# A hybrid retention / gated DeltaNet layer: the conditioning stage without GpSimd, with a matmul plan in slots, and the first value product in one pass

## The chip, the cores and the metric

The kernel runs on one core of a Trainium2 chip. The metric is the time of one execution on the device in microseconds, the median of several runs. The engines are TensorE (PE; its weight loads are listed as PEld), VectorE (DVE), ScalarE (ACT), GpSimd (POOL) and SyncE (SP), whose queue issues most of the transfers.

## The reference

One decoder layer on x of 1024 tokens by 2048 features, all in f32. Cut to what matters here:

```python
mod = silu(c) @ w_ada + b_ada                 # w_ada 2048 x 6144
shift, scale, gate = split(mod, 3)
hin = x * (1 + scale) + shift
proj = hin @ w_in                             # w_in 2048 x 7184
r_q, r_k, r_v, r_g, g_qkv, g_g, g_a, g_b = split(proj)
ret_out = groupnorm(retention(rot(r_q), rot(r_k), r_v)) * silu(r_g)         # 4 heads
gdn_out = rmsnorm(gated_delta(conv_silu(g_qkv), g_a, g_b)) * silu(g_g)      # 8 heads
y = concat(ret_out, gdn_out) @ w_out
out = layernorm(2 ** 0.25 * x + gate * y)
```

## The kernel before

Every large product keeps f32 precision with three matmuls in a faster format: an operand is split into a rounded part (`hi`, a cast on ACT) and its rest (`lo`, a subtraction), and hi x hi, hi x lo and lo x hi are summed in PSUM.

**The conditioning stage** (L139 to L356) makes the modulated input, transposed, in 16 blocks `kt` of 128 features, and does a part of `proj` beside it. The order is written out by hand for every engine (`manual_schedule`), in a loop of steps `s_`. In step `s_`:

- `load_w` brings the shift and scale columns of `w_ada` for block `s_`: four tiles `wa` of four rows `r` each, 256 KB per transfer, seven buffers. `load_x` brings the block of `x` for the next step (two buffers). All are issued by SP.
- `accumulate` (L196) forms silu(c)-weighted sums on DVE: 16 products of 128x256 (`NV = 16`), each added to one of two accumulators, and one closing sum of both (L205). Four products (`NS`) come first, the others are spread over six slots of the step.
- `reduce` (L207) sums the accumulator over its 128 partitions on PE, by a matmul with a column of ones for shift and one for scale. `modulate` (L214) adds the bias on DVE (L217, it waits for the reduction), scales `x` on ACT (L221), casts `h_hi` on ACT (L222) and subtracts to `h_lo` on POOL (L223). It works on block `s_ - 1`: in steps 1 and 2 ahead of the products, later after the first slot.
- `transpose_x` (L227) turns the block of `x` by eight PE transposes, in slots 1 and 3.
- `first_mms` (L267) does items of `proj`. An item is one block `kt` of one of two groups of columns: group 0 is `RG` (second half), `GK` and 272 columns of `RV` with the two DeltaNet gates, the latter for two of eight token tiles; group 1 is `RQ`, `RK` and `RG` (first half). An item has three tiles `t`, 18 matmuls. `TURNS` says in which order the groups use the three PSUM tiles; at the end of a turn `evict` copies the sums out (ACT) or adds them to those of an earlier turn (DVE, L298). Items are taken at `RATE = 2.0` a step, at the earliest two steps behind their block. `load_item` and `split_item` bring and split an item's weights ahead of it: the cast on ACT, the rest `w_lo` on POOL (`split` with `G`, L95), three weight buffers.

Step 16 holds two items and a last step four, all behind the last block's sum.

**After the stage**, `gemm_v(0, ...)` (L440) finishes the 272 value and gate columns for the token tiles 2 to 7. It does so in two passes of three tiles, each over all 16 blocks; each pass loads and splits the same weights in eight units (`w_unit`, L98, the rest on DVE), and uses two PSUM tiles of two banks. The evicted parts of the stage go through gates, convolution and rotary embedding on DVE, ACT and POOL meanwhile. Then follow the eight DeltaNet heads and three more retention heads: `gemm_cm` (L435) and `gemm_v` for the products, with the heads' small work spread between the matmuls, and the output product (L1065).

## Time and profile before

| | us |
|---|---|
| median of 3 runs | 1992.31 (1990.45 to 1999.22) |
| the profiled execution | 1987.55 |
| its span | 1985.7 |
| PE busy | 1879.0 (95%) |
| DVE busy | 1186.3 (60%) |
| ACT busy | 559.7 (28%) |
| POOL busy | 260.2 (13%) |

The span is the time from the first to the last instruction. A transfer counts as issued by a queue and landed later; the DMA share is the mean busy share of the 16 DMA engines, and a share above 1 occurs because packets overlap. A wait for several things is put down to the one that came last. PEclk is the granted TensorE clock: 1.00 is 2.4 GHz and 0.50 is 1.2 GHz. Successive matmuls overlap, so the price of one in a row is read from the start of one to the start of the next.

### The profile page before, as it was taken

Reading aid. Unit: us, or ns where it says so; the run is one execution under the profiler, and the core shown is the slowest. Engines: PE = TensorE matmul, PEld = TensorE weight load, DVE = VectorE, ACT = ScalarE, POOL = GpSimd, SP = SyncE. Lnnn points to the kernel's source line nnn. Section 1 sums busy time; section 2 is a strip of 40 time slices with the busy share of each in tenths; the row PEclk is TensorE's granted clock in tenths of the full one; section 3 lists DMA queues with packets and bytes.
Section 4 is the critical chain, followed back from the end, with each engine's and each line's share of the span. In section 5 each row is a group of like instructions: output and inputs, shape, how many; then the busy total and the mean of one; then the engine's idle time right before and its main releaser. Section 6 shows DMA issues by size and latency. Waiting matters only on the chain.

```text
span 1985.7 us, 28065 instructions
## 1 busy us (share of the span) xinstructions
PE 1879.0 (95%) x10272; PEld 1579.6 (80%) x10272; DVE 1186.3 (60%) x2950; ACT 559.7 (28%) x1251; POOL 260.2 (13%) x214
## 2 busy tenths in 40 slices
PE   4888899999999999999999999999999999998996
PEld 3766777787888878787878898898898878886885
DVE  7997646666575757475575752544542534458557
ACT  2433223332323232322323231211211232224221
POOL 2445202000000010000000010010010100005102
PEclk9899999999999999999999999999999999999998
DMA  9997322222221213222221241144141167345532
GB/s 272 265 262 202 114 71 72 59 67 59 59 60 51 72 49 77 49 68 58 70 58 47 72 135 52 42 146 131 43 133 49 46 206 234 118 139 176 189 111 91
DMA packets 296811, 212.29 MB, mean 107 GB/s; under 512 B 46985, under 2 KB 256474, under 8 KB 295906
## 3 DMA queue, kind: packets, MB, share of 16 engines
q1 hardware_dynamic: 294050, 202.12, 36.0%
q0 software_dynamic: 2624, 8.39, 1.2%
q8 instruction: 80, 1.31, 0.3%
q14 instruction: 57, 0.47, 0.1%
HBM read 191.54 MB, written 18.92 MB: 106 GB/s over the span
## 4 chain that ended last, share of the span: by engine, by line
PE 74%; DMA 6%; DVE 4%; issue 2%; POOL 1%; ACT 1%; SPq 0%; ACTq 0%; DVEq 0%; POOLq 0%
PE pg L435 44%; PE po L1065 14%; PE pg L468 7%; DMA gb<-gc_d 4%; DMA graw<-in_w_ada_dram 1%; DMA mixed<-mxr 1%; PE ps L753 1%; PE ps L896 1%; PE ps L563 1%; PE ps L890 1%; POOL z L1121 1%; POOL yc L877 1%; PE ps L562 1%; PE ps L912 1%; PE ps L911 1%
## 5 line engine op out<-in xcount | busy, mean ns | idle before, releaser
L435 PE MATMUL pg<-h_hi,w_hi 128*128 128x512 f32 x1376 | 451.9, 400 | 0.2 <-DVE gab L480 0.2
L435 PE MATMUL pg<-h_hi,w_lo 128*128 128x512 f32 x1376 | 449.3, 400 | 0.1
L435 PE MATMUL pg<-h_lo,w_hi 128*128 128x512 f32 x1376 | 448.3, 400 | 0.0
L94 ACT CAST w_hi<-w_raw 128x512 fp32r<-128x512 f32 (+3 forms) x244 | 150.2, 616 | 646.9 <-PE pg L435 451.2
L1065 PE MATMUL po<-wr,ms 128*128 128x512 f32 x1380 | 319.2, 393 | 8.2 <-DVE wr L1012 5.7
L1065 PEld LDWEIGHTS po<-wr,ms 128*128 128x128 f32 x1380 | 260.7, 189 | 64.8 <-DVE wr L1012 7.5
L435 PEld LDWEIGHTS pg<-h_hi,w_hi 128*128 128x128 f32 x1376 | 256.5, 189 | 49.3 <-ACT w_hi L94 1.7
L435 PEld LDWEIGHTS pg<-h_hi,w_lo 128*128 128x128 f32 x1376 | 256.9, 189 | 48.6 <-DVE w_lo L95 1.1
L435 PEld LDWEIGHTS pg<-h_lo,w_hi 128*128 128x128 f32 x1376 | 257.6, 189 | 47.6
L95 DVE TENSOR_TENSOR w_lo<-w_raw,w_hi 128x512 fp32r<-128x512 f32 (+1 forms) x211 | 150.3, 713 | 218.0 <-ACT w_hi L94 213.2
L1012 DVE TENSOR_TENSOR wr<-raw,wr 128x512 fp32r<-128x512 f32 x116 | 88.2, 763 | 111.8 <-ACT wr L1010 106.7
L468 PE MATMUL pg<-w_lo,h_hi 128*128 128x256 f32 (+1 forms) x480 | 138.1, 288 | 6.2 <-DVE w_lo L95 6.2
L468 PE MATMUL pg<-w_hi,h_hi 128*128 128x256 f32 (+1 forms) x480 | 138.7, 289 | 3.1 <-ACT w_hi L94 2.5
L468 PE MATMUL pg<-w_hi,h_lo 128*128 128x256 f32 (+1 forms) x480 | 137.9, 287 | 0.0
L201 DVE SCALAR_TENSOR_TENSOR acc<-wa,cs,acc 128x256 f32<-128x256 f32 x224 | 125.8, 623 | 4.2 <-DMA wa<-in_w_ada_dram 3.7
L1010 ACT CAST wr<-raw 128x512 fp32r<-128x512 f32 x116 | 71.8, 621 | 160.0 <-PE po L1065 148.8
L468 PEld LDWEIGHTS pg<-w_lo,h_hi 128*128 128x128 f32 x480 | 92.2, 192 | 7.6 <-DVE w_lo L95 7.5
L468 PEld LDWEIGHTS pg<-w_hi,h_hi 128*128 128x128 f32 x480 | 92.2, 192 | 6.1 <-ACT w_hi L94 4.9
L468 PEld LDWEIGHTS pg<-w_hi,h_lo 128*128 128x128 f32 x480 | 92.2, 192 | 0.0
L626 DVE SCALAR_TENSOR_TENSOR yc<-pg,cw,yc 128x1023 f32<-128x1023 f32 (+2 forms) x69 | 88.3, 1279 | 2.9 <-ACT yc L623 1.9
L415 DVE SCALAR_TENSOR_TENSOR gacc<-graw,cs,gacc 128x512 f32<-128x512 f32 x60 | 47.4, 790 | 49.4 <-DMA graw<-in_w_ada_dram 48.5
L223 POOL TENSOR_TENSOR h_lo<-xT,h_hi 128x1024 fp32r<-128x1024 f32 x16 | 48.9, 3057 | 91.4 <-ACT h_hi L222 79.0
(242 smaller groups left out, 2356.3 us busy)
## 6 DMA issues: line engine op xcount, KB each, us to landing
w_raw<-in_w_in_dram SPq DMA_DIRECT2D x212, 256.0 KB
wa<-in_w_ada_dram SPq DMA_DIRECT2D x128, 256.0 KB
raw<-in_w_out_dram SPq DMA_DIRECT2D x128, 256.0 KB
graw<-in_w_ada_dram SPq DMA_DIRECT2D x64, 256.0 KB
xs<-in_x_dram SPq DMA_DIRECT2D x16, 512.0 KB
gb<-gc_d SPq DMA_DIRECT2D x32, 256.0 KB
raw<-mixed SPq DMA_DIRECT2D x32, 256.0 KB
z<-in_x_dram SPq DMA_DIRECT2D x32, 256.0 KB
```

The costliest lines, as they stand in the source:

```text
L94: S.copy(hi[:, :n], raw[:, :n])
L95: (eng_l or V).tensor_tensor(out=lo[:, :n], in0=raw[:, :n], in1=hi[:, :n].bitcast(F32), op=ALU.subtract)
L201: V.scalar_tensor_tensor(out=a, in0=wr, scalar=cs[:, r:r + 1], in1=zero.broadcast_to([P, 2 * P]) if r < 2 else a, op0=ALU.mult, op1=ALU.add)
L223: G.tensor_tensor(out=h_lo, in0=xT, in1=h_hi.bitcast(F32), op=ALU.subtract)
L415: V.scalar_tensor_tensor(out=a, in0=raw[:, :512], scalar=cs[:, r:r + 1], in1=a, op0=ALU.mult, op1=ALU.add)
L435: PE.matmul(pt[:, i * 512:(i + 1) * 512], w[:, kk], hh[:, i * 512:(i + 1) * 512], start=(kt == 0 and w is hi and hh is hH[kt]), stop=(kt = ...
L468: PE.matmul(dst(tt), hh[:, tsl], w[:, kk], start=(kt == 0 and first_in_bank and hh is hH[kt] and w is hi), stop=(kt == KT - 1 and hh is hL ...
L562: PE.matmul(po[:, :DV], q[:, cl], state, start=True, stop=False)
L626: V.scalar_tensor_tensor(out=y[:, s:], in0=pt[:, :T - s], scalar=cw[:, j * 24 + ti:j * 24 + ti + 1], in1=y[:, s:], op0=ALU.mult, op1=ALU.add)
L1010: S.copy(t[:, :512], raw)
L1012: V.tensor_tensor(out=t[:, 512:], in0=raw, in1=t[:, :512].bitcast(F32), op=ALU.subtract)
L1065: PE.matmul(pts[tt], m[:, a + tt * P:a + (tt + 1) * P], w, start=(n == 0 and a == 0 and w is wh), stop=(n == KT - 1 and a == 512))
```

## The change

1. `NV` becomes 14: two of the 16 products of a block are not formed on DVE. `reduce` adds them on PE, with the weight tile itself as the stationary operand and the column of silu(c) as the moving one, two more matmuls for shift and two more for scale.
2. POOL does nothing in the stage: `h_lo` and all `w_lo` are subtracted on DVE, at places given in the order: a weight rest at the end of the slot in which its cast was issued, `h_lo` at the end of slot 2 (steps 1 to 3: ahead of the slots).
3. `modulate` comes ahead of the products in steps 1 to 3 rather than 1 and 2.
4. Five turns replace seven, and items are planned by tile in six slots a step (a slot is one tile of six matmuls; the third tile of group 0 counts 0.6). A block may be used one step behind, from slot 3 on. Worked out, steps 1 to 4 and step 12 hold one item, steps 5 to 8 and 13 to 15 two of group 1, steps 9 to 11 seven tiles of group 0 each, and step 16, now the last, two items of group 1 and four of group 0.
5. `gemm_v(0, ...)` runs once over all blocks for six token tiles: four PSUM banks as before and two single banks from the small pool (`small_ps`). Its weights are loaded and split once.

```diff
-    RATE = 2.0
-    TURNS = ((1, 0, 3), (0, 0, 5), (1, 3, 8), (0, 5, 11), (1, 8, 13), (0, 11, 16), (1, 13, 16))
+    TURNS = ((0, 0, 4), (1, 0, 8), (0, 4, 12), (1, 8, 16), (0, 12, 16))
+    SLOTS, SLOT, LATE = 6, 1.38, 3
...
-        NV = 16
+        NV = 14
...
-                PE.matmul(pm[:, s:s + 1], a[:, s * P:(s + 1) * P], ones[:, 0:1], start=True, stop=True)
+                for r in range(NV, 16):
+                    PE.matmul(pm[:, s:s + 1], was[kt][r // 4][:, r % 4, s], cs[:, r:r + 1], start=r == NV, stop=False)
+                PE.matmul(pm[:, s:s + 1], a[:, s * P:(s + 1) * P], ones[:, 0:1], start=False, stop=True)
...
-            G.tensor_tensor(out=h_lo, in0=xT, in1=h_hi.bitcast(F32), op=ALU.subtract)
             hH.append(h_hi)
             hL.append(h_lo)
+            return lambda: V.tensor_tensor(out=h_lo, in0=xT, in1=h_hi.bitcast(F32), op=ALU.subtract)
...
         def split_item(n):
-            if n in raws:
-                splits[n] = split(raws.pop(n), (528, 384, 544)[items[n][0]], G)
+            if n not in raws:
+                return lambda: None
+            raw, m = raws.pop(n), (528, 384, 544)[items[n][0]]
+            hi = wp.tile([P, WU], F32R, name="w_hi", tag="w_hi")
+            lo = wp.tile([P, WU], F32R, name="w_lo", tag="w_lo")
+            splits[n] = hi, lo
+            S.copy(hi[:, :m], raw[:, :m])
+            return lambda: V.tensor_tensor(out=lo[:, :m], in0=raw[:, :m], in1=hi[:, :m].bitcast(F32), op=ALU.subtract)
...
-                if kt < 5:
+                if items[n][3] == 1:
...
+        todo = [(n, t) for n in range(len(items) - 1) for t in range(3)]
+        plan = []
+        for s_ in range(KT + 1):
             plan.append([])
-            while done < len(items) - 1 and s_ >= 2 and items[done][1] <= s_ - 2 and (
-                    s_ > KT or done < max(1, (s_ - 2) * RATE)):
-                plan[s_].append(done)
-                done += 1
+            at = 0.0
+            while todo and s_:
+                n, t = todo[0]
+                grp, kt = items[n][:2]
+                if kt == s_ - 1:
+                    at = max(at, LATE)
+                if kt > s_ - 1 or (s_ < KT and at > SLOTS - 1 + 0.2):
+                    break
+                plan[s_].append((int(at), n, t))
+                todo.pop(0)
+                at += 0.6 if grp == 0 and t == 2 else 1
+        assert not todo
...
+            if s_ == 1:
+                lo0 = split_item(0)
+            if 1 <= s_ <= 3:
+                h_rest = modulate(s_ - 1, reduce(s_ - 1))
             if s_ < KT:
                 accumulate(s_, 0, NS)
             if s_ == 0:
                 use_params(*prm)
             if s_ == 1:
-                split_item(0)
-            todo = [(n, t) for n in plan[s_] for t in range(3)]
-            m = max(6, len(todo))
-            for i in range(m):
-                if i < len(todo):
-                    n, t = todo[i]
+                lo0()
+            if 1 <= s_ <= 3:
+                h_rest()
+            h_rest = None
...
+            for i in range(max([SLOTS] + [e[0] + 1 for e in plan[s_]])):
+                held, evicts[:] = evicts[:], []
+                rests = []
+                for _, n, t in [e for e in plan[s_] if e[0] == i]:
                     if t == 0:
-                        split_item(n + 1)
+                        rests.append(split_item(n + 1))
                         load_item(n + 3)
-                    held = evicts[:]
-                    evicts.clear()
                     first_mms(n, t)
-                    now = evicts[:]
-                    evicts[:] = held
-                    evict()
-                    evicts[:] = now
-                elif evicts:
-                    evict()
-                if i == 0 and 3 <= s_ <= KT:
-                    modulate(s_ - 1, reduce(s_ - 1))
-                if s_ < KT:
-                    accumulate(s_, NS + i * (NV - NS) // 6, NS + (i + 1) * (NV - NS) // 6)
+                now, evicts[:] = evicts[:], held
+                evict()
+                evicts[:] = now
+                if i == 0 and 4 <= s_ <= KT:
+                    h_rest = modulate(s_ - 1, reduce(s_ - 1))
+                if s_ < KT and i < SLOTS:
+                    accumulate(s_, NS + i * (NV - NS) // SLOTS, NS + (i + 1) * (NV - NS) // SLOTS)
                     if i in (1, 3):
                         transpose_x(s_, i // 2)
+                for f in rests:
+                    f()
+                if i == LATE - 1 and h_rest:
+                    h_rest()
...
-        per_bank = 1 if gab is not None else 2
-        for tts in ((2, 3, 4), (5, 6, 7)) if gab is not None else (range(NC),):
-            pts = [pg.tile([P, T], F32, name="pg", tag="pg") for _ in range(2)]
-            def dst(tt):
-                j = tt - tts[0]
-                o = j % (2 * per_bank) * (512 // per_bank)
-                return pts[j // (2 * per_bank)][:, o:o + n]
-            for u in range(KT // 2):
-                if gab is not None and u == 0 and tts[0] == 2:
-                    hi, lo = (w[:, :2 * n].rearrange("p (a n) -> p a n", n=n) for w in ahead)
-                else:
-                    hi, lo = w_unit(w3[:, 2 * u:2 * u + 2, RV + r * DV:RV + (r + 1) * DV], 2, n,
-                                    None if gab is None else w3[:, 2 * u:2 * u + 2, GA:GA + 16])
-                if r > 1:
-                    gate_unit()
-                    gate_unit()
-                for half in (tts[:2 * per_bank], tts[2 * per_bank:]):
-                    for kk in range(2):
-                        for tt in half:
-                            kt = 2 * u + kk
-                            tsl = slice(tt * P, (tt + 1) * P)
-                            first_in_bank = per_bank == 1 or tt % 2 == 0
-                            for hh, w in ((hH[kt], hi), (hH[kt], lo), (hL[kt], hi)):
-                                PE.matmul(dst(tt), hh[:, tsl], w[:, kk],
-                                          start=(kt == 0 and first_in_bank and hh is hH[kt] and w is hi),
-                                          stop=(kt == KT - 1 and hh is hL[kt]), skip_group_check=True)
-                                tick(0.5)
+        pts = [pg.tile([P, T], F32, name="pg", tag="pg") for _ in range(2)]
+        if gab is None:
+            tts = range(NC)
+            dsts = [pts[tt // 4][:, tt % 4 * n:(tt % 4 + 1) * n] for tt in tts]
+        else:
+            tts = range(2, NC)
+            pts += [small_ps() for _ in range(2)]
+            dsts = [t[:, o:o + n] for i, t in enumerate(pts) for o in ((0, 512) if i < 2 else (0,))]
+        for u in range(KT // 2):
+            if gab is not None and u == 0:
+                hi, lo = (w[:, :2 * n].rearrange("p (a n) -> p a n", n=n) for w in ahead)
+            else:
+                hi, lo = w_unit(w3[:, 2 * u:2 * u + 2, RV + r * DV:RV + (r + 1) * DV], 2, n,
+                                None if gab is None else w3[:, 2 * u:2 * u + 2, GA:GA + 16])
+            if r > 1:
+                gate_unit()
+                gate_unit()
+            for half in (tts[:len(tts) // 2], tts[len(tts) // 2:]):
+                for kk in range(2):
+                    for tt in half:
+                        kt = 2 * u + kk
+                        tsl = slice(tt * P, (tt + 1) * P)
+                        first_in_bank = gab is not None or tt % 2 == 0
...
+        if gab is None:
             for j in range(2):
-                if gab is None:
-                    S.copy(vt[:, 4 * j:4 * j + 4].rearrange("p t d -> p (t d)"), pts[j])
-                else:
-                    t1 = tts[0] + 2 * j
-                    m = 2 - j
-                    src = pts[j].rearrange("p (t d) -> p t d", d=512)[:, :m]
-                    S.copy(vt[:, t1:t1 + m], src[:, :, :DV])
-                    V.tensor_copy(gab[:, t1:t1 + m], src[:, :, DV:DV + 16])
+                S.copy(vt[:, 4 * j:4 * j + 4].rearrange("p t d -> p (t d)"), pts[j])
+        else:
+            for t, t1 in zip(pts, (2, 4, 6, 7)):
+                src = t.rearrange("p (t d) -> p t d", d=512)
+                m = src.shape[1]
+                S.copy(vt[:, t1:t1 + m], src[:, :, :DV])
+                V.tensor_copy(gab[:, t1:t1 + m], src[:, :, DV:DV + 16])
```

## Rows read from the trace of the kernel before

**Rows 1.** Windows view: stretch; engines' busy us (instructions), PEclk, DMA share, rate

```profile
57.00:187.00 130.00, 110.88 (x543) 89.48 (x542) 122.47 (x208) 52.60 (x71) 60.41 (x34) 0.95 0.96 259
215.00:265.40 50.40, 40.94 (x290) 38.26 (x288) 31.66 (x42) 14.54 (x25) 8.35 (x7) 0.97 0.37 104
265.40:1985.70 1720.30, 1673.38 (x9214) 1408.31 (x9214) 978.15 (x2595) 464.84 (x1118) 161.07 (x154) 0.99 0.31 90
```

**Rows 2.** DMA view, 0 to 190 us: rate by slice, packets, issues

```profile
GB/s 126 246 288 305 290 269 288 300 294 305 291 252 197 296 227 293 254 244 299 278 289 222 247 297 189 291 281 234 294 265 290 283 291 290 215 297 170 268 273 17
DMA packets 99552, 49.14 MB, mean 259 GB/s; under 512 B 6209, under 2 KB 99538, under 8 KB 99538
wa<-in_w_ada_dram SPq DMA_DIRECT2D x128, 256.0 KB
xs<-in_x_dram SPq DMA_DIRECT2D x16, 512.0 KB
```

**Rows 3.** DMA view, 57 to 187 us: packets and bytes

```profile
DMA packets 68292, 33.69 MB, mean 259 GB/s; under 512 B 4505, under 2 KB 68281, under 8 KB 68281
```

**Rows 4.** Groups by form, 0 to 230 us: count, busy us, mean ns

```profile
L201 DVE SCALAR_TENSOR_TENSOR acc<-wa,cs,acc 128x256 f32<-128x256 f32 x224 | 125.8, 623 | 4.2 <-DMA wa<-in_w_ada_dram 3.7
L223 POOL TENSOR_TENSOR h_lo<-xT,h_hi 128x1024 fp32r<-128x1024 f32 x16 | 48.9, 3057 | 91.4 <-ACT h_hi L222 79.0 <-DMA wa<-in_w_ada_dram 9.3 <-DMA colsc<-in_tab_dram 3.1
L205 DVE SCALAR_TENSOR_TENSOR acc<-acc 128x256 f32<-128x256 f32 x16 | 17.5, 1096 | 0.6
```

**Rows 5.** Timeline, DVE and POOL: start, us, engine, line, operation, count

```profile
16.18 0.42 DVE L205 SCALAR_TENSOR_TENSOR acc<-acc 128x256 f32<-128x256 f32 x1
...
41.71 4.82 DVE L201 SCALAR_TENSOR_TENSOR acc<-wa,cs,acc 128x256 f32<-128x256 f32 x12
44.29 4.45 POOL L223 TENSOR_TENSOR h_lo<-xT,h_hi 128x1024 fp32r<-128x1024 f32 x1 [4.43 <-ACT h_hi L222]
46.57 2.45 DVE L205 SCALAR_TENSOR_TENSOR acc<-acc 128x256 f32<-128x256 f32 x1
...
56.50 2.52 DVE L205 SCALAR_TENSOR_TENSOR acc<-acc 128x256 f32<-128x256 f32 x1
...
186.87 2.47 DVE L205 SCALAR_TENSOR_TENSOR acc<-acc 128x256 f32<-128x256 f32 x1
```

**Rows 6.** Timeline, PE: start, us, engine, line, operation, count

```profile
16.76 0.98 PE L211 MATMUL px<-ones,acc 128*128 128x1 f32 x4 [5.47 <-DVE acc L205]
...
184.31 0.60 PE L232 MATMUL px<-ident,xs 128*128 128x128 f32 x4
184.67 0.71 PE L281 MATMUL pg<-h_hi,w_hi 128*128 128x512 f32 x2
...
191.57 0.50 PE L211 MATMUL px<-ones,acc 128*128 128x1 f32 x4
191.94 0.75 PE L281 MATMUL pg<-h_hi,w_hi 128*128 128x512 f32 x2
...
201.97 0.28 PE L276 MATMUL pg<-w_hi,h_hi 128*128 128x272 f32 x1
...
202.72 0.63 PE L281 MATMUL pg<-h_hi,w_hi 128*128 128x512 f32 x2
...
210.92 0.61 PE L281 MATMUL pg<-h_hi,w_hi 128*128 128x512 f32 x2
...
215.00 0.28 PE L468 MATMUL pg<-w_hi,h_hi 128*128 128x272 f32 x1
```

**Rows 7.** DVE: groups by form from 57 us, and timeline near 237 us

```profile
L298 DVE SCALAR_TENSOR_TENSOR part<-pg,part 128x1024 f32<-128x1024 f32 x8 | 9.7, 1216 | 0.9 <-PE pg L281 0.9
...
237.16 0.72 DVE L95 TENSOR_TENSOR w_lo<-w_raw,w_hi 128x544 fp32r<-128x544 f32 x1
```

**Rows 8.** Waits of PE, 215 to 265.4 us: total us, times, longest

```profile
PE pg L468 <- DVE w_lo L95: 6.2, 6, 2.0
PE pg L468 <- ACT w_hi L94: 2.5, 2, 1.8
```

More of the change, by code (lines that the diff above doesn't have):

```diff
@@ L88, in hybrid_layer_kernel, with split @@
     WU = 576
-    def split(raw, n, eng_l=None):
+    def split(raw, n):
         hi = wp.tile([P, WU], F32R, name="w_hi", tag="w_hi")
@@ L94, in split @@
             S.copy(hi[:, :n], raw[:, :n])
-            (eng_l or V).tensor_tensor(out=lo[:, :n], in0=raw[:, :n], in1=hi[:, :n].bitcast(F32), op=ALU.subtract)
+            V.tensor_tensor(out=lo[:, :n], in0=raw[:, :n], in1=hi[:, :n].bitcast(F32), op=ALU.subtract)
         return hi, lo
@@ L233, in transpose_x @@
             S.copy(xTs[kt][:, i * 512:(i + 1) * 512], ph)
-        items = [(g_, kt, kt == k0, kt == k1 - 1) for g_, k0, k1 in TURNS for kt in range(k0, k1)] + [(2, 0, 0, 0)]
+        items = [(g_, kt, kt == k0, (2 if k0 else 1) if kt == k1 - 1 else 0) for g_, k0, k1 in TURNS
+                 for kt in range(k0, k1)] + [(2, 0, 0, 0)]
         ps0 = []
@@ L276, in first_mms @@
                         PE.matmul(ps0[2][:, tt * 512:tt * 512 + DV + 16], hh[:, tsl], w[:, 2 * P:2 * P + DV + 16],
-                                  start=(first and hh is hH[kt] and w is hi), stop=(last and hh is hL[kt]))
+                                  start=(first and hh is hH[kt] and w is hi), stop=bool(last and hh is hL[kt]))
             else:
@@ L282, in first_mms @@
                                   hh[:, i * 512:(i + 1) * 512],
-                                  start=(first and w is hi and hh is hH[kt]), stop=(last and hh is hL[kt]))
+                                  start=(first and w is hi and hh is hH[kt]), stop=bool(last and hh is hL[kt]))
             if last:
@@ L301, in hybrid_layer_kernel @@
         st.enter_context(tc.manual_schedule())
-        plan, done = [], 0
-        for s_ in range(KT + 2):
+        todo = [(n, t) for n in range(len(items) - 1) for t in range(3)]
+        plan = []
+        for s_ in range(KT + 1):
             plan.append([])
-            while done < len(items) - 1 and s_ >= 2 and items[done][1] <= s_ - 2 and (
-                    s_ > KT or done < max(1, (s_ - 2) * RATE)):
-                plan[s_].append(done)
-                done += 1
+            at = 0.0
[10 more added lines that the diff above has]
+        assert not todo
         load_w(0, range(1))
@@ L311, in hybrid_layer_kernel @@
         prm = load_params()
-        for s_ in range(KT + 2):
+        for s_ in range(KT + 1):
             if s_ < KT:
@@ L325, in hybrid_layer_kernel @@
             if s_ == 1:
-                split_item(0)
-            todo = [(n, t) for n in plan[s_] for t in range(3)]
-            m = max(6, len(todo))
-            for i in range(m):
-                if i < len(todo):
-                    n, t = todo[i]
+                lo0()
[6 more added lines that the diff above has]
+                for _, n, t in [e for e in plan[s_] if e[0] == i]:
                     if t == 0:
-                        split_item(n + 1)
+                        rests.append(split_item(n + 1))
                         load_item(n + 3)
-                    held = evicts[:]
-                    evicts.clear()
                     first_mms(n, t)
-                    now = evicts[:]
-                    evicts[:] = held
-                    evict()
-                    evicts[:] = now
-                elif evicts:
-                    evict()
-                if i == 0 and 3 <= s_ <= KT:
-                    modulate(s_ - 1, reduce(s_ - 1))
-                if s_ < KT:
-                    accumulate(s_, NS + i * (NV - NS) // 6, NS + (i + 1) * (NV - NS) // 6)
+                now, evicts[:] = evicts[:], held
[5 more added lines that the diff above has]
+                    accumulate(s_, NS + i * (NV - NS) // SLOTS, NS + (i + 1) * (NV - NS) // SLOTS)
                     if i in (1, 3):
                         transpose_x(s_, i // 2)
+                for f in rests:
+                    f()
+                if i == LATE - 1 and h_rest:
+                    h_rest()
         evict()
-        assert done == len(items) - 1
-        ahead = splits[done]
+        ahead = splits[len(items) - 1]
         main = ctx.enter_context(ExitStack())
@@ new lines, in gemm_v @@
+        pts = [pg.tile([P, T], F32, name="pg", tag="pg") for _ in range(2)]
[21 more added lines that the diff above has]
+                        first_in_bank = gab is not None or tt % 2 == 0
+                        for hh, w in ((hH[kt], hi), (hH[kt], lo), (hL[kt], hi)):
+                            PE.matmul(dsts[tt - tts[0]], hh[:, tsl], w[:, kk],
+                                      start=(kt == 0 and first_in_bank and hh is hH[kt] and w is hi),
+                                      stop=(kt == KT - 1 and hh is hL[kt]), skip_group_check=True)
+                            tick(0.5)
```

1 line of the change is left out of this document (removed).

## The prediction

> **What bounds the kernel now.** I read the windows of time first, because a mean over the span hides that this kernel has two regimes. From 265.4 us to the end the matrix engine (PE) is busy for 1673.4 of 1720.3 us [rows 1]; nothing of that part is edited, so the change is worth what it takes off the first 265.4 us. There PE is not the bound: between 57 and 187 us it works for 110.9 of 130 us, while VectorE (DVE) works for 122.5 [rows 1]. One step of this stage handles one of the 16 column blocks `kt` of the input. The sum of a step's products (L205) starts at 16.18 us for the first block and at 186.87 us for the last [rows 5], so a step takes 170.7 / 15 = 11.4 us on average.
>
> Next the groups by form: 224 of the 256 products take 0.623 us each, and the closing sum 1.10 us [rows 4]. The timeline says why. Twelve products that start before GpSimd (POOL) has work take 4.82 us, 0.40 each; the sum that starts at 46.57 us, in the middle of POOL's 4.45 us subtraction, takes 2.45 us instead of the 0.42 it takes at 16.18 us [rows 5]. DVE and POOL hold each other up. By the groups, 224 products lose 224 x (0.623 - 0.40) = 50 us and the sums 16 x (1.096 - 0.42) = 11 us.
>
> Last the transfers, because a faster DVE hands the bound to them. The stage moves 49.14 MB at a mean of 259 GB/s, but its third to eleventh slices lie between 269 and 305, mean 292 [rows 2]. So the queue has some 12% in hand, not more.
>
> **The change, part by part, as us per step of the stage.**
>
> DVE: 14 products at 0.40 (5.6), the sum 0.42, the rest `h_lo` of a block, two weight rests `w_lo`, and evictions. No row shows `h_lo` on DVE: the same shape from PSUM takes 1.22 us [rows 7], and POOL's own 3.06 [rows 4] is the far end, gone too far since half of it was waiting; two 544-wide rests at 0.72 [rows 7], for 1088 columns, make 1.44. I take 1.22, the nearest form. Two `w_lo` make 1.44 at most. Nine evictions add on DVE, six of them inside the steps: 6 x 1.22 / 16 = 0.5. Sum 9.2 us, against 11.4 now. With 3.06 for `h_lo` it would be 11.0.
>
> PE: an item of group 1 takes 215.00 - 210.92 = 4.08 us; the third tile of group 0 takes 202.72 - 201.97 = 0.75, so that item takes 2 x 1.36 + 0.75 = 3.47. Eight transposes take 2 x (184.67 - 184.31) = 0.72. The reduction, four instruction pairs in 191.94 - 191.57 = 0.37 us, becomes twelve: 1.11 [rows 6]. The heaviest step is 8.16 + 0.72 + 1.11 = 10.0 us. These are prices at the 2.4 GHz level; at 1.2 GHz the four pairs take 0.98 [rows 6].
>
> Transfers: 128 x 0.262 + 16 x 0.524 = 41.9 MB of conditioning weights and input, the remaining 7.2 of the 49.14 MB are mostly `w_in` [rows 2]: 3.07 MB a step, at 292 GB/s 10.5 us. The bytes are unchanged, only the order of the `w_in` blocks differs. Moved past the SP queue are the loads of an item: they still wait for the rests of the item three earlier, now on DVE instead of POOL. New is that the last quarter of a step's weights stays occupied until PE has reduced it in the next step; with seven buffers the transfer that needs this place comes seven quarters later, and I cost that at nothing, up to one step's quarter (0.5 MB, 1.8 us at 292 GB/s) once if the cover fails.
>
> So transfers (10.5) bind, PE (10.0) follows closely, DVE (9.2) falls behind both. From 57 us on 33.69 MB are left [rows 3]; at 292 GB/s that is 115.4 us, so the last products' sum ends at about 172.5 us instead of 186.87 + 2.47 = 189.3 [rows 5]: **16.8 us**. Its ends: at the best slice, 305 GB/s, 110.5 us and 21.8 us of gain; at 275, halfway between 259 and 292, 122.5 us and 9.8 of gain.
>
> First steps: in steps 1 to 3 `modulate` stands ahead of the products, so DVE waits for the reduction with nothing queued that could pass. Twelve pairs in place of four at the low clock cost 2 x 0.98 = 2.0 us a step [rows 6], 5.9 us in all at most; the transfers run ahead meanwhile. I charge **1 us**, between 0 and 5.9.
>
> Behind the stage: today 215.00 - 189.3 = 25.7 us of items follow the last sum. The new plan holds two items of group 1 and four of group 0 in its last step: 2 x 4.08 + 4 x 3.47 = 22.0 us, of which the first slot (1.36) comes ahead of the reduction. With eight pairs after the sum (0.74) and an estimated 0.5 for the wait on `h_lo`, 21.9 us: **3.8 us** saved. If the first slot isn't done in time it is 2.4.
>
> V0 in one pass: 288 matmuls of 272 columns at 0.75 / 6 = 0.125 us [rows 6] are 36.0 us, but the stretch lasts 50.4 [rows 1]; PE waits there for DVE's rests (6.2 us) and ScalarE's casts (2.5) [rows 8], and loses the rest at shorter gaps and at a granted clock of 0.97 [rows 1]. One pass loads and splits eight pairs of rows rather than sixteen, and each split covers 36 matmuls (4.5 us) instead of 18. The same evictions, gates, convolution and rotary work stand in DVE's queue beside it. I take 2 us of waiting as left, an estimate between 0 and 7 (half of today's 14.4): 38.0 us, **12.4 us** saved (7.4 to 14.4). The six output tiles take two banks of the small pool, which nothing else uses until the first head's work is spawned, so that costs nothing; if a later tile had to wait there, it would be for one eviction (1.22 us).
>
> Sum: 16.8 - 1 + 3.8 + 12.4 = 32.0 us. The span 1985.7 becomes 1953.7, the profiled execution 1987.55 becomes 1955.6. The median of the runs shown, 1992.31, lies 4.8 above that execution; taken from it, the forecast is **1960 us**.
>
> **Rivals.**
>
> *The loop binds.* DVE waits for PE's reduction in the same queue in which it holds PE's `w_lo` and `h_lo`, and PE does one item slot before it reduces. A step then costs 11.0, between PE's 10.0 and today's mean. From 56.50 us, 11 steps at 11.0 end at 178 rather than 173: 11 us gained there, with 3.8 and V0's 12.4 less 2 for a late DVE, some 25: **1968**. For it speaks how close 10.0 is to 10.5; against it, that PE's step 12 holds only one item.
>
> *The transfers are full already.* The busy share of the DMA engines is 0.96 at 259 GB/s [rows 1]. If that were the ceiling for this mix, the stage wouldn't shorten: 3.8 and V0's 7.4 to 12.4 remain, 11 to 16 us: **1978**. Against it, the nine slices at 292.
>
> *PE binds because the transfers have more in hand.* If DVE alone has held the queue back, a step costs PE's 10.0: 11 of them, less 4 us for the single-item step, end at 163 to 165 us, some 8 us better than the sum: **1952**. Against it, no slice goes above 305. The Trainium skill (DMA: Bandwidth & Descriptors, section Bandwidth, Measured) gives 341 GB/s for transfers of 1 MB and 425 for 16 MB; by 341 the 33.69 MB would take an estimated 98.8 us, and the sum would be PE's. No slice here shows such a rate.
>
> *Slower: PE at the 1.2 GHz level.* A full step then costs PE 20.0 us, nearly twice the transfers. Between 57 and 187 us the mean granted clock is 0.95 [rows 1]; at that mean PE's step is 10.0 / 0.95 = 10.5, which costs nothing yet. Today's steps from 56.5 us on average 130.4 / 11 = 11.85 us. To eat what is gained outside the steps (15 us) they must average 11.85 + 15 / 11 = 13.2 us, a mean clock of 0.76; to be slower by 10 us, 14.1, a clock of 0.71: **2003**. For it: the first four steps hold one item each, about half of PE's time; against it, from step 5 on PE has more than 8 us of work in nearly every 10.5. The Trainium skill (TensorE: Matmul & The Clock Gate, Part 1) says that the low rate is the default and that activity of the array releases it; by that rule it is these four light steps that are at risk, while the rows here show no single cause for the drops.
>
> **How the numbers follow.** Forecast 0.55, loop 0.19, full transfers 0.11, PE-bound 0.07, half clock 0.05, and 0.03 for a time near today's because V0's single pass brings nothing and the loop loses what the sum gives. A measurement of this kernel can tell about 0.5% (10 us) from no change. Faster by more: 0.85; within: 0.09 (the 0.03 and half of the worst of the full-transfer case); slower: 0.06. The range runs from 1950 (sum with 21.8 for the stage and 14.4 for V0, 40 us) to 1980 (nothing from the stage, 7.4 from V0, no luck behind it), which leaves out about 0.15.
>
> **What would show it.** In the profile after: no POOL row in the first 170 us, products at 0.40 and sums at 0.42; steps of 10.4 to 10.6 us, transfers near 290 GB/s throughout; the last sum ending near 172; the reduction at 1.1 us a step; the first V0 matmul at 195 and the first matmul of the next product at 233. If the products are 0.40 but DVE idles behind the reduction, the loop rival holds. If the rate stays at 259 with DVE idle for data, the transfers were full. If V0 still takes over 43 us, the one pass wasn't the cure for its waits. The prediction is wrong as a whole if the stretch from 265.4 us on, shifted, isn't as long as now (1720 us).

## The result, and the profile after

The changed kernel takes 1977.41 us (median; 1975.30 to 1979.25) against 1991.38 for the kernel before: a ratio of 0.9922, interval 0.9893 to 0.9951. That is 14 us, where 32 were forecast. The profiled execution takes 1977.74 us, its span 1976.0. The two spans differ by 9.7 us only, since the profiled execution of before lies 3.8 us below its median. Cut where the prediction cut, in us:

```
                                    before   forecast    after
end of the last block's sum          189.3      173.5    186.8
from there to V0's first matmul       25.7       21.9     25.0
V0                                    50.4       38.0     41.4
from there to the end               1720.3     1720.3   1722.8
span                                1985.7     1953.7   1976.0
```

Of the 22.3 us missing in the span, 13.3 are in the stage, 3.1 behind it, 3.4 in V0 and 2.5 in the untouched part. For these 2.5 no run shows a cause; in the runs below the same part takes between 1721.5 us (v0_two) and 1733.2 (w_on_pool).

The windows view of after (stretch; busy us of PE, PEld, DVE, ACT, POOL with instructions; PEclk; DMA share; GB/s), for the stretches of [rows 1]; the last line is V0:

```profile
57.00:187.00 130.00, 121.26 (x635) 100.95 (x635) 99.69 (x220) 54.49 (x74) 0.00 (x0) 0.95 0.99 262
211.76:253.20 41.44, 38.72 (x290) 38.05 (x289) 26.57 (x34) 10.45 (x18) 8.86 (x7) 0.96 0.28 81
```

DVE's 122.5 us have become 99.7 and POOL's work is gone, yet the rate has moved from 259 to 262 GB/s only. The groups by form of after, 57 to 187 us, say that each instruction got as short as forecast (compare [rows 4]), and what DVE does instead:

```profile
L201 DVE SCALAR_TENSOR_TENSOR acc<-wa,cs,acc 128x256 f32<-128x256 f32 x137 | 59.1, 481 | 2.8 <-DMA wa<-in_w_ada_dram 1.9 <-DVE mod L219 0.7
L227 DVE TENSOR_TENSOR h_lo<-xT,h_hi 128x1024 fp32r<-128x1024 f32 x12 | 14.7, 1223 | 0.1
L201 DVE SCALAR_TENSOR_TENSOR acc<-wa,cs,zero 128x256 f32<-128x256 f32 x22 | 9.7, 481 | 18.7 <-DMA wa<-in_w_ada_dram 18.7
L205 DVE SCALAR_TENSOR_TENSOR acc<-acc 128x256 f32<-128x256 f32 x12 | 5.1, 425 | 0.4
```

The third line is the finding: the first products of a block (input `zero`) stand 18.7 us for weights that haven't arrived. The steps, from one start of L205 to the next, show where (worked out from the timelines of DVE; the number is the block's):

```
step             1    2    3    4    5    6    7    8    9   10   11   12   13   14   15   last sum starts
before        11.9 11.0  7.5  9.9 16.6 10.6 12.1 10.6 14.0 12.1 11.5 11.5  7.7 15.7  8.0   186.87
after         14.4 10.0 10.4 10.0 10.9 10.5 10.5 11.8 12.4 15.6 10.9 14.8  8.9  9.5 10.5   186.38
w_on_pool     10.8 10.0 10.0  9.1 10.9 10.5 10.5 10.6 11.5 15.1  8.4 13.0  8.9  9.5 10.5   176.98
pool_alog     10.8 10.5 10.0  8.9 11.3 10.5 10.5 10.6 11.5 11.6  9.5 12.9  8.9  9.5 10.5   174.83
w_merge       14.3 10.0 10.1  8.9 11.1 10.5 10.5 10.7 12.0 12.8 10.4 13.5  8.9  9.5 10.5   179.36
half_w        11.6 10.0 10.0  8.2 11.5 10.5 10.5 10.6 11.5 12.7  9.5 12.1  8.9  9.5 10.5   172.76
```

After's ordinary step is the 10.5 us that the prediction gave, though for another reason (see half_w). Five long ones (1, 8, 9, 10, 12) spoil it. Step 10 is the worst, and the timeline of SyncE's DMA queue in after shows why (start, us, line, tile, number of loads):

```profile
96.48 0.78 SPq L186 DMA_DIRECT2D xs<-in_x_dram  x1
97.36 5.70 SPq L262 DMA_DIRECT2D w_raw<-in_w_in_dram  x8
103.11 5.64 SPq L192 DMA_DIRECT2D wa<-in_w_ada_dram  x8
108.85 0.71 SPq L186 DMA_DIRECT2D xs<-in_x_dram  x1
109.65 7.45 SPq L262 DMA_DIRECT2D w_raw<-in_w_in_dram  x12
117.14 5.66 SPq L192 DMA_DIRECT2D wa<-in_w_ada_dram  x8
```

The rows join with gaps of 0.1 us at most. Twelve loads of projection weights (three items of group 0) hold the list for 7.45 us, and only then come the conditioning weights of the next block, 14.0 us behind those of the block before. The rate by slices of 1.125 us between 90 and 135 us of after falls to 79 GB/s near 116 us (24th slice) and, one block earlier, to 64 near 104 (13th); DVE then waits for 4.54 us:

```profile
GB/s 271 115 304 290 279 314 283 303 289 290 236 162 64 301 237 264 308 306 290 292 295 281 180 79 177 189 285 253 311 267 258 301 305 299 231 124 234 314 265 281
```

```profile
116.63 0.70 DVE L275 TENSOR_TENSOR w_lo<-w_raw,w_hi 128x528 fp32r<-128x528 f32 x1
121.87 0.88 DVE L201 SCALAR_TENSOR_TENSOR acc<-wa,cs,zero 128x256 f32<-128x256 f32 x2 [4.54 <-DMA wa<-in_w_ada_dram]
```

The same view of before, which the prediction did not read, has the same list without gaps:

```profile
34.40 5.13 SPq L192 DMA_DIRECT2D wa<-in_w_ada_dram  x8
39.64 1.03 SPq L186 DMA_DIRECT2D xs<-in_x_dram  x1
40.77 3.08 SPq L259 DMA_DIRECT2D w_raw<-in_w_in_dram  x4
43.95 5.38 SPq L192 DMA_DIRECT2D wa<-in_w_ada_dram  x8
...
103.94 5.29 SPq L192 DMA_DIRECT2D wa<-in_w_ada_dram  x8
109.34 0.65 SPq L186 DMA_DIRECT2D xs<-in_x_dram  x1
110.40 6.16 SPq L259 DMA_DIRECT2D w_raw<-in_w_in_dram  x8
116.65 5.24 SPq L192 DMA_DIRECT2D wa<-in_w_ada_dram  x8
```

Four loads of projection weights stand between two blocks near 40 us (a round of 9.55 us), eight near 110 us (12.7 us). The slices at 292 GB/s that the prediction took for the queue's reserve [rows 2] lie between 9.5 and 52 us, where the list is still short.

### The profile page after: what moved, and what is told of

Its sections match the earlier page's. It is cut to its first block, busy times and chain, and to the rows that moved or that the text cites. A ratio compares the mean times of both kernels' runs of the same rounds, so it can differ in the third digit from the quotient of the medians.

```text
span 1976.0 us, 28123 instructions
## 1 busy us (share of the span) xinstructions
PE 1890.5 (96%) x10400; PEld 1595.4 (81%) x10400; DVE 1154.2 (58%) x2953; ACT 554.6 (28%) x1243; POOL 168.4 (9%) x165
## 4 chain that ended last, share of the span: by engine, by line
PE 73%; DMA 4%; DVE 4%; issue 1%; ACT 1%; POOL 1%; SPq 0%; DVEq 0%; ACTq 0%; POOLq 0%
PE pg L457 44%; PE po L1086 15%; PE pg L489 6%; DMA gb<-gc_d 3%; DMA graw<-in_w_ada_dram 1%; PE ps L774 1%; PE ps L933 1%; PE ps L917 1%; PE ps L911 1%; POOL z L1142 1%; PE ps L932 1%; PE ps L923 1%; PE ps L584 1%; PE ps L583 0%; PE ps L574 0%
## 5 line engine op out<-in xcount | busy, mean ns | idle before, releaser
L457 PE MATMUL pg<-h_hi,w_hi 128*128 128x512 f32 x1376 | 451.9, 400 | 0.0
L94 ACT CAST w_hi<-w_raw 128x512 fp32r<-128x512 f32 (+1 forms) x203 | 126.1, 621 | 598.2 <-PE pg L457 440.6
L95 DVE TENSOR_TENSOR w_lo<-w_raw,w_hi 128x512 fp32r<-128x512 f32 (+1 forms) x203 | 143.1, 705 | 211.6 <-ACT w_hi L94 206.9
L489 PE MATMUL pg<-w_lo,h_hi 128*128 128x256 f32 (+1 forms) x448 | 128.6, 287 | 2.3 <-DVE w_lo L95 2.3
L489 PE MATMUL pg<-w_hi,h_hi 128*128 128x256 f32 (+1 forms) x448 | 128.9, 288 | 0.4 <-DVE part L308 0.4
L489 PE MATMUL pg<-w_hi,h_lo 128*128 128x256 f32 (+1 forms) x448 | 128.7, 287 | 0.0
L489 PEld LDWEIGHTS pg<-w_lo,h_hi 128*128 128x128 f32 x448 | 86.2, 192 | 2.8 <-DVE w_lo L95 2.7
L489 PEld LDWEIGHTS pg<-w_hi,h_hi 128*128 128x128 f32 x448 | 86.2, 192 | 2.5 <-ACT w_hi L94 1.7
L489 PEld LDWEIGHTS pg<-w_hi,h_lo 128*128 128x128 f32 x448 | 86.2, 192 | 0.0
L201 DVE SCALAR_TENSOR_TENSOR acc<-wa,cs,acc 128x256 f32<-128x256 f32 x192 | 82.2, 481 | 4.5 <-DMA wa<-in_w_ada_dram 3.4
L291 PE MATMUL pg<-h_hi,w_hi 128*128 128x512 f32 x160 | 57.9, 445 | 17.0 <-ACT h_hi L224 14.7
```

Source lines behind the costliest of these rows:

```text
L94: S.copy(hi[:, :n], raw[:, :n])
L95: V.tensor_tensor(out=lo[:, :n], in0=raw[:, :n], in1=hi[:, :n].bitcast(F32), op=ALU.subtract)
L201: V.scalar_tensor_tensor(out=a, in0=wr, scalar=cs[:, r:r + 1], in1=zero.broadcast_to([P, 2 * P]) if r < 2 else a, op0=ALU.mult, op1=ALU.add)
L291: PE.matmul(ps0[t][:, i * 512:(i + 1) * 512], w[:, t * P:(t + 1) * P], hh[:, i * 512:(i + 1) * 512], start=(first and w is hi and hh is hH ...
L457: PE.matmul(pt[:, i * 512:(i + 1) * 512], w[:, kk], hh[:, i * 512:(i + 1) * 512], start=(kt == 0 and w is hi and hh is hH[kt]), stop=(kt = ...
L489: PE.matmul(dsts[tt - tts[0]], hh[:, tsl], w[:, kk], start=(kt == 0 and first_in_bank and hh is hH[kt] and w is hi), stop=(kt == KT - 1 an ...
```

## The experiments

Three theories of what held the stage at 187 us. **Queue**: SyncE issues all loads in one list, in order; the loads of projection weights stand ahead of the next block's conditioning weights. **Full transfers**: 262 GB/s is all that this mix of transfers gives. **PE**: its waits and low clock. All ratios are to the kernel before.

A few profiled executions (`w_on_pool`, `raw4`, `pool_nv16_turns`) lie 7 to 11 us above their medians, the excess mostly behind V0; stages are read from the trace, times from the median.

**w_on_pool**: the projection weights' loads go through GpSimd's queue.

```diff
-                nc.sync.dma_start(out=raw[:, o:o + n_], in_=w3[:, kt, c0:c0 + n_])
+                nc.gpsimd.dma_start(out=raw[:, o:o + n_], in_=w3[:, kt, c0:c0 + n_])
```

> The changed kernel, with the w_in loads of the conditioning stage issued by POOL's queue instead of SP's; bytes, order and everything else as they are. Queue theory: the five long steps (14.4, 11.8, 12.4, 15.6 and 14.8 us against 10.4 for the others) come from SP's queue, where up to twelve w_in loads, some waiting for a weight buffer, stand ahead of the next block's conditioning weights. Then steps 8 to 10 fall to 10.5 to 11 and the last sum ends some 8 us earlier, at about 179 us; time 1966 to 1971. Full-transfers theory: 262 GB/s is what this mix gets; the last sum stays at 187 (185 to 189), time 1975 to 1980. PE theory (PE's waits and its low clock make the long steps): also no change, 1975 to 1980, and the long steps stay where they are.

1967.69 us, ratio 0.9885 (0.9848 to 0.9922); the last sum starts at 176.98, 9.4 us earlier. The windows view, 60 to 140 us, of after and then of w_on_pool:

```profile
60.00:140.00 80.00, 75.62 (x404) 62.77 (x402) 57.70 (x129) 36.63 (x49) 0.00 (x0) 0.98 1.00 265
```

```profile
60.00:140.00 80.00, 76.04 (x425) 64.16 (x424) 62.72 (x143) 37.41 (x51) 28.12 (x53) 0.99 1.13 297
```

The same transfers run at 297 GB/s: full transfers are refuted, and with them the DMA busy share as a sign of a ceiling, since it read 1.00 at 265 GB/s. Steps 1 and 8 are mended, 9 and 12 in part; step 10 is not. ScalarE's timeline of w_on_pool names another in-order queue:

```profile
110.74 0.63 ACT L274 CAST w_hi<-w_raw 128x528 fp32r<-128x528 f32 x1 [0.16 <-DVE acc L201]
118.39 0.21 ACT L668 ACTIVATE alog<-alog 128x8 f32<-128x8 f32 x1 [7.02 <-DMA alog<-in_gdn_a_log_dram]
118.51 1.23 ACT L223 ACTIVATE xT<-xT,mod 128x1024 f32<-128x1024 f32 x1
```

With SyncE's list shorter, the scheduler puts small constants of a later stage into this one, and ScalarE stands 7.02 us on one of them ahead of the block's activations. Their factors were ready on DVE at 114.87, so 3.6 us are lost.

**pool_alog**: w_on_pool, and that exponential is made to depend on the last gate values.

```diff
+        V.scalar_tensor_tensor(out=alog, in0=gab[:, 7, 0:8], scalar=0.0, in1=alog, op0=ALU.mult, op1=ALU.add)
         S.activation(out=alog, in_=alog, func=AF.Exp)
```

> The loads of the projection weights are issued by GpSimd (as in w_on_pool) and the exponential of the decay constants (L668) is made to follow the last gate values, so that ScalarE cannot block on it inside the stage. Queue theory: the 7 us for which ScalarE stood in step 10 of w_on_pool go, the step falls from 15.1 to about 10.5, the last sum starts near 172.5 instead of 176.98, and the time is about 1963 us (w_on_pool 1967.7). Rival (that step is long because PE and DVE are late, ScalarE only shows it): last sum stays near 177, time 1968.

Step 10 falls to 11.6 us, about as the queue theory expected (10.5); steps 9, 10 and 12 stay above 10.5, so the last sum starts at 174.83, not 172.5. The time is 1966.39 us (ratio 0.9870, 0.9855 to 0.9884). From w_on_pool's median that is 1.3 us, within the scatter: the step is shown, its time is not.

**w_early**: all loads on SyncE, but from block 5 on the next block's conditioning weights stand ahead of the projection weights.

```diff
-            if s_ < KT:
+            if s_ < 4 or s_ == 4:
...
+                if i == 0 and 4 <= s_ < KT - 1:
+                    load_w(s_ + 1)
+                if i == 3 and 4 <= s_ < KT - 2:
+                    load_x(s_ + 2)
```

> The changed kernel, with the conditioning weights of the next block issued on SP right behind slot 0 of a step from step 4 on (the input block behind slot 3), so ahead of the later w_in loads of that step; all stays on SP. Queue theory: the same gain as by moving the w_in loads away, less what the w_in loads now come late: last sum at 179 to 184 us, time 1967 to 1974. Full-transfers and PE theory: 1975 to 1980.

1974.64 us (ratio 0.9903, 0.9874 to 0.9932), last sum at 183.49: another order within one list wins back 2.9 us of the stage, a second list 9.4. The time lies just above the 1967 to 1974 of the queue theory, and its runs overlap with those of after.

**raw4**: after with four buffers for raw projection weights instead of three.

```diff
-            if n % 3 < 2:
+            if n % 4 < 2:
...
-                raw = sp.tile([P, 544], F32, name="w_raw3", tag="w_raw3", bufs=1)
+                raw = sp.tile([P, 544], F32, name="w_raw3", tag="w_raw3", bufs=2)
```

> The kernel after with four buffers instead of three for the raw projection weights; all loads stay on SyncE in the same order. If SyncE's queue stands because a load waits for its buffer to come free, the long steps 1, 8, 9 and 10 shrink by most of their 12.4 us together: last sum near 176 to 180 instead of 186.4, time 1967 to 1971. If it is the number of loads ahead (up to twelve at some 0.45 us each), not the buffer, nothing moves: last sum 184 to 187, time 1975 to 1979.

Last sum at 186.19, 1974.99 us (0.9910, 0.9893 to 0.9926). SyncE's timeline of raw4:

```profile
109.74 7.42 SPq L262 DMA_DIRECT2D w_raw<-in_w_in_dram  x12
117.21 5.52 SPq L192 DMA_DIRECT2D wa<-in_w_ada_dram  x8
```

The twelve loads take 7.42 us instead of 7.45. My first explanation, a load that waits for its weight buffer, falls. By the waits view, the waits within those 7.45 us of after sum to 2.8, and to 2.4 in raw4, so the fourth buffer doesn't remove them; what they are for stays open. The rest, some 0.4 us for each load, is issuing.

**w_merge**: after, with two of an item's column blocks in one DMA: 80 loads instead of 112, the same bytes.

```diff
-                cols = ((RG + P, P), (GK, P), (RV, DV), (GA, 16))
+                cols = ((RG + P, P, GK - RG - P), (RV, DV, 0), (GA, 16, 0))
...
-                cols = ((RQ, P), (RK, P), (RG, P))
+                cols = ((RQ, P, RK - RQ), (RG, P, 0))
```

> The kernel after, with two of the column blocks of each item loaded by one DMA instead of two: 80 loads of projection weights from the stage instead of 112, same bytes, same queue (SyncE), same order, same buffers. Issue theory: SyncE works through its list without a gap from 57 to 187 us, at some 0.43 us a load plus waits, and sets the stage; 32 loads less take 10 to 14 us from it until TensorE binds: last sum at 174 to 179 instead of 186.4, time 1964 to 1970. Rival (the bytes, or the wait for a free weight buffer, hold the queue): last sum within 2 us of 186.4, time 1975 to 1979.

1969.61 us (0.9871, 0.9842 to 0.9900), last sum at 179.36, 7.0 us earlier at the same bytes, queue and buffers. This shows the queue theory by itself: only the number of loads in the list has changed. SyncE's timeline of w_merge, the block of step 10:

```profile
106.28 1.66 SPq L265 DMA_DIRECT2D w_raw<-in_w_in_dram  x1
107.99 0.93 SPq L267 DMA_DIRECT2D w_raw<-in_w_in_dram  x2
109.02 0.38 SPq L265 DMA_DIRECT2D w_raw<-in_w_in_dram  x1
109.45 0.94 SPq L267 DMA_DIRECT2D w_raw<-in_w_in_dram  x2
110.54 0.38 SPq L265 DMA_DIRECT2D w_raw<-in_w_in_dram  x1
111.58 0.80 SPq L267 DMA_DIRECT2D w_raw<-in_w_in_dram  x2
112.43 6.07 SPq L192 DMA_DIRECT2D wa<-in_w_ada_dram  x8
```

Nine loads hold the list from 106.28 to 112.43, 6.15 us, and step 10 is 12.8 us long instead of 15.6. Where it doesn't wait, a load of two pieces is issued in 0.38 us, no longer than one of one piece. The first load of the block takes 1.66: a wait that a shorter list doesn't remove.

**before_merge**: the same edit in the kernel before.

> The kernel before with the same 32 loads merged away, nothing else changed. If SyncE's list set the stage of before too, its last sum (186.9 there) comes 3 to 10 us earlier, as far as VectorE (122 us busy of 130) and TensorE let it, and the time falls by as much, to 1981 to 1988. If the stage of before was set by VectorE's shared work (products 0.62, sums 1.1) or by the rate of the transfers, its last sum stays within 2 us and the time within 3 us of before.

1986.74 us (0.9972, 0.9953 to 0.9992), last sum at 182.19 instead of 186.87. So SyncE's list set the stage of before too, for 4.7 us; behind that VectorE probably binds, busy 115.5 of the 118 us from 57 to 175 there.

**g_back**: after, with `h_lo` and `w_lo` back on GpSimd.

```diff
-            return lambda: V.tensor_tensor(out=h_lo, in0=xT, in1=h_hi.bitcast(F32), op=ALU.subtract)
+            return lambda: G.tensor_tensor(out=h_lo, in0=xT, in1=h_hi.bitcast(F32), op=ALU.subtract)
```

(and the same for `w_lo`)

> The kernel after with the two low halves (of the activations, L227, and of the projection weights, L275) back on GpSimd; everything else as after. If GpSimd's work is what made the products 0.62 us long and the sums 1.1, products go from 0.48 back to about 0.6 and sums to about 1.0, VectorE's step is 14 x 0.6 + 1.0 + 0.1 = 9.5 us against 9.2 now, each low half of the activations takes 3 us instead of 1.2, and the last sum comes at 187 to 195: time 1978 to 1986. If the stage's length is set by transfers held in SyncE's queue alone, the last sum stays within 2 us of 186.4 and the time within 3 us of 1977.

1980.43 us (0.9948, 0.9933 to 0.9962), last sum at 188.06. The groups by form of g_back, 57 to 175 us:

```profile
L201 DVE SCALAR_TENSOR_TENSOR acc<-wa,cs,acc 128x256 f32<-128x256 f32 x118 | 79.4, 736 | 4.2 <-DMA wa<-in_w_ada_dram 3.3 <-DVE mod L219 0.5
L227 POOL TENSOR_TENSOR h_lo<-xT,h_hi 128x1024 fp32r<-128x1024 f32 x10 | 26.4, 2640 | 41.5 <-ACT h_hi L224 35.5 <-DMA wa<-in_w_ada_dram 6.1
L205 DVE SCALAR_TENSOR_TENSOR acc<-acc 128x256 f32<-128x256 f32 x10 | 6.3, 635 | 0.3
```

Its last sum, in DVE's timeline:

```profile
188.06 2.50 DVE L205 SCALAR_TENSOR_TENSOR acc<-acc 128x256 f32<-128x256 f32 x1
```

GpSimd's subtractions do make the products long (0.736 against 0.481), but that costs the stage 3.8 us (the last sum's end, 190.6 against 186.8). The medians differ by 3.0 us, and the two intervals overlap. While the list sets the stage, freeing VectorE is worth little.

**half_w**: two of four conditioning weight tiles of a block (from block 1 on) aren't loaded; the first stands for them.

```diff
+                if kt and rh in (1, 2):
+                    was[kt].append(was[kt][0])
+                    continue
```

> The changed kernel with two of the four weight tiles of each block (from the second block on) not loaded; the first tile is read three times instead, so the sums leave half of the conditioning weights out. Every instruction on DVE, PE and ACT is as before; 15.7 MB less are moved. Full-transfers and queue theory alike: steps fall to what PE and DVE need, 10.0 at most where two items stand in a step, 9 or less in light ones: last sum at 150 to 165 us, span 1940 to 1955. PE theory: the long steps stay, last sum above 178, span above 1965.

1961.1 us in one execution, last sum at 172.76, later than the 150 to 165 that I expected from queue and transfers and earlier than the 178 of the PE theory. This leaves out 60 loads and 15.7 MB together, so it doesn't part the two; it shows where the stage ends with neither in the way. The windows view, 57 to 175 us, and PE's timeline of half_w in an ordinary step:

```profile
57.00:175.00 118.00, 114.43 (x623) 96.86 (x622) 94.09 (x208) 53.15 (x73) 0.00 (x0) 0.99 0.66 177
```

```profile
79.58 0.51 PE L215 MATMUL px<-cs,wa 128*128 128x1 f32 x4
...
80.84 0.71 PE L294 MATMUL pg<-h_hi,w_hi 128*128 128x512 f32 x2
81.39 0.62 PE L294 MATMUL pg<-h_hi,w_lo 128*128 128x512 f32 x2
81.85 0.62 PE L294 MATMUL pg<-h_lo,w_hi 128*128 128x512 f32 x2
...
90.08 0.50 PE L215 MATMUL px<-cs,wa 128*128 128x1 f32 x4
```

PE is busy 114.4 of 118 us, and its step is 90.08 - 79.58 = 10.50: the reduction takes 1.26 (to 80.84; I had 1.11), and the pair behind it 0.55 instead of 0.46. PE binds where I had put the transfers, so that the forecast of 10.5 us for a step came true is luck.

**pool_nv16**: pool_alog with all sixteen products on VectorE.

```diff
-        NV = 14
+        NV = 16
...
-                PE.matmul(pm[:, s:s + 1], a[:, s * P:(s + 1) * P], ones[:, 0:1], start=False, stop=True)
+                PE.matmul(pm[:, s:s + 1], a[:, s * P:(s + 1) * P], ones[:, 0:1], start=NV == 16, stop=True)
```

> pool_alog with all sixteen products on VectorE and only the sum on TensorE. TensorE loses 0.9 us a step of 10.5 (eight of the twelve matmuls of the reduction), VectorE gains two products of 0.45. If TensorE binds the steps, the step is about 9.7 to 10.2 and the last sum comes 3 to 8 us before that of pool_alog. If VectorE is as near (its step 9.2 plus 0.9 = 10.1, with waits on top), nothing is won: within 2 us of pool_alog, or up to 8 us later.

1962.77 us (0.9854, 0.9839 to 0.9869), the fastest that loads all weights, 3.6 below pool_alog, though the two intervals overlap. Ordinary steps fall from 10.5 to 9.6, so PE did bind them; but steps 8, 10 and 12 take 11.7, 13.0 and 13.3 (in step 10 DVE waits 2.3 us for conditioning weights), and the last sum starts only 0.5 us earlier. The rest lies behind it: PE arrives less late (23.3 us to V0 instead of 25.0), and V0 runs at a granted clock of 1.00:

```profile
198.07:237.88 39.81, 37.08 (x290) 36.41 (x289) 26.59 (x34) 10.45 (x18) 8.93 (x7) 1.00 0.30 85
```

**pool_nv16_turns**: pool_nv16 with the turns cut at block 11, so that step 12 holds two items instead of one.

```diff
-    TURNS = ((0, 0, 4), (1, 0, 8), (0, 4, 12), (1, 8, 16), (0, 12, 16))
+    TURNS = ((0, 0, 4), (1, 0, 8), (0, 4, 11), (1, 8, 16), (0, 11, 16))
```

> pool_nv16 with the turns cut at block 11 instead of 12, so that the two items of block 11 fall apart and step 12 is no longer the one with a single late item (13.3 us there, with TensorE at a mean granted clock of 0.77 in the same stretch of after). If the light step is what lets TensorE fall behind, step 12 shrinks to 10 to 11 us and the last sum comes 2 to 3 us earlier: time 1959 to 1961 (pool_nv16 1962.8). If it is VectorE's evictions that cost the time there, they only move to another step: last sum within 1 us, time 1962 to 1964.

Neither theory: step 12 falls from 13.3 to 9.6 us, but step 11 grows from 9.6 to 11.3, step 15 from 8.9 to 10.6, the last sum starts at 174.87, and 27.8 us follow it instead of 23.3, at a clock of 0.94. 1971.47 us (0.9881, 0.9846 to 0.9915). The light step moved to step 15, and step 16 has no item of an earlier block left to begin with: PE stands 2.66 us there for `h_hi` of the last block, and the granted clock is 0.81 from 174.87 to 184.00. What step 12 gained is lost there.

In after the light step 12 takes 14.8 us. Of these 2.7 go with the loads (12.1 in half_w). The windows view and PE's timeline of after show what else happens in it:

```profile
143.00:158.00 15.00, 10.79 (x53) 8.83 (x51) 10.57 (x22) 4.29 (x6) 0.00 (x0) 0.77 1.11 293
```

```profile
149.30 1.22 PE L291 MATMUL pg<-h_hi,w_hi 128*128 128x512 f32 x2 [4.12 <-ACT h_hi L224]
```

The step's only item needs the block that is made in the same step, so PE stands 4.12 us for `h_hi`; the granted clock is 1.00 up to 145.20, ahead of that wait, and 0.52 from 149.30 to 155.30, behind it. The wait comes first, and the low clock follows.

**v0_two**: after, with `gemm_v` as in the kernel before; its core:

```diff
-            tts = range(2, NC)
+        for tts in ((2, 3, 4), (5, 6, 7)) if gab is not None else (range(NC),):
```

> The changed kernel with the first value product in two passes again (the function as it was before). It tells the worth of the one pass apart from the stage. By the profiles, V0 takes 41.4 us now and took 50.4: 9 us slower than the changed kernel, 1984 to 1989. If the evictions of the new last turn make two passes wait less than they did, 1980 to 1984.

1989.08 us (0.9985, 0.9973 to 0.9997). V0 takes 52.7 us instead of 41.4. So the one pass, put on top of the other edits, is worth 11.7 of the change's 14 us, and all of the stage's edits without it some 2. Two passes took 50.4 us in before; for the 2.3 more no run shows a cause, and the one pass on top of before was not run.

## Why the prediction was wrong

**The bound** is the step that failed. "A faster DVE hands the bound to them", the transfers, with "some 12% in hand": the bytes had that reserve, SyncE's list had not. The sentence that costed this at nothing is "they still wait for the rests of the item three earlier": it asks whether one load waits, not how long the list is. Eight conditioning loads and eight to twelve projection loads at 0.6 to 0.8 us a load make a round of 12 to 14 us (short waits included), above PE's 10.5. That is the stage's 13.3 missing us: w_merge gives back 7.0 of them by fewer loads, pool_alog 11.6 by a second list and without ScalarE's wait. The forecast 173.5 is about the least that PE allows: half_w, without 60 of the 128 conditioning loads, ends its last sum at 173.2, and there PE sets the stage. The Trainium skill (Perfetto Trace Analysis, section What "DMA-bound" means) counts a solid track of DMA slices on the issuing engine as one of three ways to be bound by DMA. This case's rows agree, in before as in after, and the prediction read only one of the three. The Trainium skill (DMA: Bandwidth & Descriptors, section Issuing engines are not separate DMA queues) says that issuing from several engines saves only the issue time, usually small beside the transfer. The measurement differs: here saving it took the rate from 265 to 297 GB/s and 9.7 us off the time.

**The rival that came true in time only.** "The transfers are full already" gave 1978, and 1977.4 was measured, with the share near 1 and DVE idle for data as that rival asked. w_on_pool shows that its mechanism is false all the same. The sign that I named (259 GB/s with DVE idle) can't tell a full transfer from a late issue; SyncE's row points to the second, and w_on_pool decides.

**VectorE and GpSimd.** Right in mechanism and price: h_lo 1.223 us on DVE (1.22 predicted), sums 0.425 (0.42); products are 0.40 in a run and 0.48 alone. Wrong in worth: g_back, with GpSimd back, loses 3.8 of the 16.8 us that were forecast for the stage. The 50 us that the products were said to lose set a length (0.623) against a spacing (0.40); against the undisturbed length, 0.48, they are 32. And three of the nine evictions fall into the steps, not six.

**PE's step.** 10.5 measured, 10.0 predicted: the twelve pairs take 1.26 us, and at each switch from reduction or transposes to products the first pair takes 0.55 instead of 0.46.

**The tail**, 25.0 instead of 21.9. PE's timeline of after:

```profile
186.39 0.61 PE L291 MATMUL pg<-h_hi,w_hi 128*128 128x512 f32 x2
...
189.11 0.50 PE L212 MATMUL px<-cs,wa 128*128 128x1 f32 x4
...
190.37 0.71 PE L291 MATMUL pg<-h_hi,w_hi 128*128 128x512 f32 x2
```

The sum ends at 186.8, but PE starts the reduction at 189.11, 2.3 us later: the first slot isn't done by then, a case that the prediction priced at 1.4. PE has not even begun that slot; the last slot of step 15 is still running. In all, PE is busy for 24.9 of the 25.0 us.

**V0**: 41.4 us, forecast 38.0. The cure was right (PE's waits for `w_lo` there are 2.3 us, 6.2 in [rows 8]), the size was off: PE has 37.1 us of work, not 36.0, waits are 2.7, and at a granted clock of 0.96 the stretch takes 1.6 us more than the 39.8 at 1.00 in pool_nv16 and w_merge. The waits view of after:

```profile
PE pg L489 <- DVE w_lo L95: 2.3, 2, 2.1
```

**First steps.** Step 1 takes 14.4 us, 10.8 in w_on_pool. DVE and ScalarE in after:

```profile
26.88 0.63 ACT L274 CAST w_hi<-w_raw 128x528 fp32r<-128x528 f32 x1 [5.92 <-DMA w_raw<-in_w_in_dram]
27.55 0.71 DVE L275 TENSOR_TENSOR w_lo<-w_raw,w_hi 128x528 fp32r<-128x528 f32 x1 [2.88 <-ACT w_hi L274]
```

Here the projection weights themselves are late. They are issued from 20.60 us on, behind the conditioning weights of their step, and DVE waits for their cast. So it is their place in the list, not its length: in w_merge, with a shorter list, the step still takes 14.3. The reduction that I charged 1 us for isn't what sets step 1 apart, but it is dearer than that: in w_on_pool DVE waits 2.0 us for it in step 1 and 1.1 in each of steps 2 and 3, and steps 2 and 3 stay at 10.0, in half_w too.

## What to carry to other kernels

Before a faster engine is counted on to feed from transfers, read the issuing engine's row: if its loads join without a gap, the list may bound the stage, whatever the rate. The row alone doesn't prove it, since waits stand inside its lengths (31 of the 130 us from 57 to 187 in after); merging some loads at the same bytes does. Merge loads, or give the projection weights a queue of their own, before engines are unburdened; then look what a shorter list lets the scheduler pull forward into an in-order queue. And a rate taken as the reserve must come from a stretch with the same list of loads.

## What the runs showed of the hardware

A load's price on SyncE hardly follows its bytes or pieces: in w_merge 0.38 us for 128 KB in two pieces, 0.93 for two loads of 128 and 8 KB, and in after a median of 0.51 for 256 KB. The busy share of the DMA engines read 1.00 at 265 GB/s and 1.13 at 297, so it is no ceiling. Issuing a load of projection weights takes 0.53 us on GpSimd (median of 112) and 0.43 on SyncE, and moving them still gained 9.7 us. V0's 290 matmuls keep PE busy for 37.1 us at a granted clock of 1.00 and 38.7 at 0.96. In after the clock fell from 1.00 to 0.52 behind a wait of 4.12 us.
